# Six pairs instead of four in five output chunks of a one-layer encoder, with the last norm's weight row in its own tile

## The chip, the cores and the metric

The kernel runs on one core of one Trainium2 chip (trn2). The core's engines run side by side, each with its own in-order list of instructions, and wait for each other through semaphores: TensorE (PE, matmuls, with its weight loads as PEld), VectorE (DVE), ScalarE (ACT), GpSimd (POOL) and SyncE (SP), which issues nearly all DMAs. The metric is the device time of one execution in microseconds; lower is better.

## The reference

One layer: an embedding norm, one large input projection, two branches (a gated short convolution and banded window attention), one output projection, and a norm over the sum with the scaled stream. All in float32, 256 tokens by 4096 columns.

```python
h = layer_norm(x, emb_ln_g, emb_ln_b)
p = h @ w_in                       # 4096 x 13312
y_conv = c_b * centred_short_conv(c_c * c_h, conv_w) * silu(c_z)
y_attn = banded_window_attention(a_q, a_k, a_v, sink) * silu(a_z)
y = concatenate([y_conv, y_attn]) @ w_out      # 4096 x 4096
out = layer_norm(2 ** 0.25 * h + y, ln_g, ln_b)
```

## The kernel before, in words

**Two halves of a number.** TensorE multiplies rounded float32. To keep precision, each weight and each activation is split into a high half (rounded) and a low half (the rest), and three products are summed: high by high, activation's low by weight's high, activation's high by weight's low. ScalarE writes a weight's high half `whi` (line 226), VectorE its low half `wlo` (line 230), and TensorE takes both.

**Steps.** The whole work is one list of steps, `steps`, built from strings (lines 45 to 49). A letter `s` is a *piece*: 4 row blocks of 128 weights by 512 columns, 1 MB, 32 matmuls with the high half and 16 with the low (`mm_out`, line 957, in the output projection). A letter `S` is a *pair*: 2 row blocks by 512 columns, 0.5 MB, multiplied by a scheme of seven products instead of eight (`mm_pair`, lines 300 to 303): 14 matmuls with high halves and 7 with low. Four row blocks are thus one piece (48 matmuls) or two pairs (42). A pair costs more elsewhere: sums of its weight blocks on VectorE (`sums`, lines 192 to 194 for two neighbouring pairs in one go, 205 to 207 for a single one), sums of the activations for its row blocks, made once for all chunks (`x_sums`, called from `y_sums`), and a combination of the products at the end of the chunk (`pair_sums`, lines 709 to 712).

**Coupled pairs.** Two pairs that stand next to each other in the list are a couple. Both their weights lie in the four slots of the tile `wall`, and their sums are one set of three instructions (lines 192 to 194) that needs both loads. A couple may not use the extra load buffers that lie in the result tile `R` (R0 and R1 up to chunk 4, R2 in chunks 5 and 6); pieces and single pairs may.

**The output projection.** 4096 columns are nine chunks, numbered 0 to 8: seven of 512 columns, two of 256. Chunks 0 and 1 are eight pieces each, chunks 2 to 6 follow the string `sSsSsSsSss`, chunks 7 and 8 are pieces. In this document a chunk's steps are counted from 0.

**What one step issues, in this order.** For step j: its matmuls; on ScalarE the high halves of step j + 3; whatever is due `later`; then `loads(j)` puts weight loads up to seven steps ahead on SP, each waiting until its buffer's last user is split; on VectorE the block sums of step j + 4 if that is a pair, then the low halves of step j + 3. There are three buffers for high halves and three for low ones, so both of step j + 3 wait for TensorE to be through with step j. Behind these come, in certain steps of a chunk: the residual (`residual`, lines 938 and 940: the stream's norm for the chunk's columns), the product with the last norm's weight row for the chunk before (`end_out2`, line 979), and the loads of the residual's rows (`res_load`, lines 928 to 932). After the last step comes the chunk's end (`end_out`, lines 972 to 975: sum and statistics).

**The last norm's rows.** In step 4 of chunk 2 `rows_load` fetches the last norm's weights and biases; in step 8 `rows_split` splits them on VectorE (lines 904 and 905) and sends them with 15 small DMAs on SP (line 908) to the tile `rows`, used at the very end.

Of the kernel before, what the change touches and what calls it, by code (L numbers as in the profile page):

```python
# [8 lines left out]
F32 = mybir.dt.float32  # L9
F32R = mybir.dt.float32r  # L10
AF = mybir.ActivationFunctionType
ALU = mybir.AluOpType
AX = mybir.AxisListType

P = 128
# [26 lines left out]
HT = S // 2  # L42
# [2 lines left out]
PAIRS = [0, 0, NP1] + [NP] * (len(IN_ORDER) - 3)  # L45
ORDERS = {0: "s" * 8, NP1: "sssSSsSsSs", NP: "sSSsSSSSsSSs"}
OUT = 100
OP = 4
OUT_ORDERS = ["s" * 8] * 2 + ["sSsSsSsSss"] * 5 + ["", ""]
N_W = 4  # L50
OFF = 4
GAP = 64
# [20 lines left out]
def out_units(n):  # L73

    if CHUNKS[n] < W:
        return [("out", OUT + n, q) for q in range(KT * CHUNKS[n] // PIECE)]
    q, p, us = 2 * npairs(OUT + n) // PK, 0, []
    for u in OUT_ORDERS[n]:
        if u == "s":
            us.append(("out", OUT + n, q))  # L80
            q += 1
        else:
            us.append(("opair", OUT + n, p))
            p += 1
    assert q == NPC
    return us


def npairs(ci):
    return PAIRS[ci] if ci < OUT else OUT_ORDERS[ci - OUT].count("S")  # L90

# [3 lines left out]
N_IN = len(IN_STEPS)  # L95
# [6 lines left out]
def encoder_kernel(ctx: ExitStack, tc: tile.TileContext, x, emb_g, emb_b, wi, ws, conv_w, sink, wo, ln_g, ln_b, out):  # L102
    nc = tc.nc
# [14 lines left out]
    steps = IN_STEPS + OUT_STEPS  # L118
    chunks = []
# [4 lines left out]
    def couple(j):  # L124
# [5 lines left out]
    psc = pw = pc = R = None  # L130
    extra = []
    user = {}
    in_R = [(steps.index(("opair", OUT + 4, OP - 1)) + 1, "R0"), (steps.index(("opair", OUT + 4, OP - 1)) + 1, "R1"),
            (steps.index(("opair", OUT + 6, OP - 1)) + 1, "R2")]

    def w_bufs(j):

# [86 lines left out]
    def split_hi(j):  # L224
        wh[j] = half_tile(j, "whi")
        nc.scalar.activation(part(j, wh[j]), part(j, raw[j]), AF.Copy)  # L226
# [24 lines left out]
    for name in ("whi", "wall", "wlo0", "m", "nm", "wlo1", "den", "es", "wlo2"):  # L251
        n = {"whi": PIECE + GAP}.get(name, PIECE + 2 * OFF if name[:3] == "wlo" else N_W * PIECE if name == "wall" else 2)
        t = wpool.tile([P, n], F32, name=name, bufs={"whi": 3, "m": 4, "nm": 3, "den": 4, "es": 3}.get(name, 1))
# [25 lines left out]
    pacc, SC = {}, None  # L279
# [211 lines left out]
    SC = [sc_tiles[p // (NP - 3)][:, p % (NP - 3), :, :, :] for p in range(NP)]  # L491
# [208 lines left out]
    def pair_copy(ci):  # L700
        e = st_["e", ci] = sum_tile(ci)
        nc.scalar.activation(e[:, 0, 0:HW], pacc[ci, 0][:, 0, :], AF.Copy)
# [86 lines left out]
    def at(j, fn, *a):  # L789
        later.setdefault(j, []).append((fn, a))  # L790
# [71 lines left out]
    ncs = len(chunks)  # L862
    res = {}
    p2 = st2 = ms2 = rows = t5 = lhs5 = None
    RB = [(0, 0), (0, 1), (0, 2), (32, 0), (32, 1), (32, 2), (64, 0), (64, 1)]

    def bcast(src, a, n):
        return bass.AP(tensor=src.tensor, offset=src.offset + a, ap=[[0, P], [1, n]])
# [22 lines left out]
    def z_tile():  # L891
        if not zt:
            zt.append(p2.tile([P, 12 * W], F32, name="z", tag="SC"))
        return zt[0]
# [15 lines left out]
    def res_load(n):  # L910
        if n >= ncs:
            return
        c0, w, _, _ = chunks[n]
        if n < ncs - 1:
            gb = p2.tile([P, 3, w], F32, name="gb")
        if n < ncs - 2:
            xc = p2.tile([P, 2, W], F32, name="xc")[:, :, 0:w]
        elif n == ncs - 2:
            xc = z_tile()[:, 6 * W:6 * W + 2 * w].rearrange("p (a b) -> p a b", a=2)
        else:  # L920
            z = zt[0]
            gb = z[:, 0:3 * w].rearrange("p (a b) -> p a b", a=3)
            xc = z[:, 3 * w:5 * w].rearrange("p (a b) -> p a b", a=2)
            g1, b1, t1 = (z[:, 5 * w + k * W:5 * w + (k + 1) * W] for k in range(3))
            first_cols.extend((g1, b1, t1, z[:, 5 * w + 3 * W:5 * w + 3 * W + P]))
            nc.sync.dma_start(out=g1, in_=bcast(ln_g, 0, W))
            nc.sync.dma_start(out=b1, in_=bcast(ln_b, 0, W))
        nc.sync.dma_start(out=gb[:, 0, :], in_=bcast(emb_gr, c0, w))
        nc.sync.dma_start(out=gb[:, 1, :], in_=bcast(emb_br, c0, w))
        nc.sync.dma_start(out=gb[:, 2, :], in_=bcast(ln_g, c0, w))  # L930
        for i in range(2):
            nc.sync.dma_start(out=xc[:, i, :], in_=x[i * P:(i + 1) * P, c0:c0 + w])
        res[n] = gb, xc

    def residual(n):
        gb, xc = res[n]
        for i in range(2):
            nc.vector.scalar_tensor_tensor(xc[:, i, :], xc[:, i, :], musd[:, i, 0:1], gb[:, 0, :],
                                           op0=ALU.subtract, op1=ALU.mult)
            nc.vector.scalar_tensor_tensor(xc[:, i, :], xc[:, i, :], musd[:, i, 2:3], gb[:, 1, :],  # L940
                                           op0=ALU.mult, op1=ALU.add)
# [34 lines left out]
        return r  # L976

    def end_out2(n, i, r):
        nc.vector.tensor_tensor(r, r, res[n][0][:, 2, :], op=ALU.mult)

    def finish_lhs(n, i):
        r = end_out(n, i)
# [53 lines left out]
    def y_sums(k):  # L1036
        nonlocal SC
        if k == 0:
            t = p2.tile([P, 6, 2, 4, HT], F32R, name="SCy", tag="SC")
            SC = [t[:, p, :, :, :] for p in range(OP)]  # L1040
        x_sums(k, R[:, 0, 2 * W:4 * W])

    for k in range(OP):
        at(chunks[1][3] + 1 + k, y_sums, k)
    ends = []
    for n, (c0, w, pk, j0) in enumerate(chunks):
        us = out_units(n)
        np_ = sum(u[0] == "opair" for u in us)
        for t, (kind, _, q) in enumerate(us):
            j = j0 + t  # L1050
            if kind == "opair":
                mm_pair(j)
            else:
                mm_out(j, n, (0,) if n == ncs - 1 else (0, 1))
            if j + 3 < len(steps):
                split_hi(j + 3)
            for fn, a in later.pop(j, []):
                fn(*a)
            if kind == "opair" and q == np_ - 1:
                pair_copy(OUT + n)  # L1060
                at(j + 1, pair_sums, OUT + n)
                at(j + 1, plus_res, n)
            if j == N_IN + 5:
                open_p2()
            loads(j)
            if j == N_IN + 5:
                res_load(0)
            sums(j + 4)
            if j + 3 < len(steps):
                split_lo(j + 3)  # L1070
            if t == 0 and n:
                for a in ends:
                    end_out2(*a)
                ends = []
                if n < ncs - 1:
                    res_load(n)
            if t == (0 if n == ncs - 1 else 2 if n == ncs - 2 else 4 if n else 7):
                residual(n)
            if n == 2 and t == 4:
                rows_load()  # L1080
            if n == 2 and t == 8:
                rows_split()
                nc.scalar.activation(small.tile([P, 1], F32, name="sd", bufs=1), eps_t, AF.Abs_reciprocal_sqrt)
            if n == ncs - 2 and t == 1:
                res_load(ncs - 1)
        if n < ncs - 1:
            ends = [(n, i, end_out(n, i)) for i in range(2)]
    assert not later
    last_mm = chunks[-1][3]
    n = ncs - 1  # L1090
# [78 lines left out]
```

## Time and profile before

| | |
|---|---|
| median of 3 runs | 1501.05 us (1500.09 to 1501.15) |
| profiled execution | 1500.92 us |
| its span, first to last instruction | 1499.2 us |
| TensorE busy | 1482.4 us |
| VectorE busy | 1338.4 us |
| ScalarE busy | 803.3 us |
| output chunk 2 begins, chunk 3 begins | 1229.7 us, 1271.9 us |

How to read the profile: a row of the order of time gives start and length in us, engine, line, operation, what it writes and reads, and in square brackets the idle time of the engine before it and what ended that. A row of a stretch gives, engine by engine, busy us and the number of instructions; then TensorE's granted clock as a share of full speed, the mean busy share of the 16 DMA engines, and GB/s. A row of a group gives busy us, the mean ns of one, and idle time before it. SPq is SP's queue: its rows are the issuing of DMAs, not their transfer.

### The profile page before, as it was taken

The numbers are of one execution on the slowest core, as the hardware profiler recorded it, in microseconds if no ns is written. First come the engines' busy times: TensorE is split into PE (matmuls) and PEld (weight loads), VectorE is DVE, ScalarE is ACT, GpSimd is POOL, SyncE is SP. The second block draws the span as 40 slices with busy tenths as digits, with TensorE's granted clock in tenths as the row PEclk, the third lists the DMA queues.
The fourth block names the chain that finished last, engine by engine and source line by source line (L and its number), as shares of the span: only waits on it lengthen the run. The fifth ranks groups of instructions, "written<-read, shape, count | busy, mean of one in ns | idle before, by whom it ended". The sixth has DMA issues, their size and how long they took to land.

```text
span 1499.2 us, 29810 instructions
## 1 busy us (share of the span) xinstructions
PE 1482.4 (99%) x12878; PEld 1465.4 (98%) x12878; DVE 1338.4 (89%) x1384; ACT 803.3 (54%) x687; POOL 1.3 (0%) x7
## 2 busy tenths in 40 slices
PE   7999999999999999999999999999999999999998
PEld 4999999999999999999999999999999999999997
DVE  7768999898999999999999999999998688888876
ACT  5544656766666665655555555555555444444431
POOL 0000000000000000000000000000000000000000
PEclk9999999999999999999999999999999999999999
DMA  8545465555554556646545655556558656756663
GB/s 318 217 183 196 164 217 189 192 197 208 180 204 176 190 201 209 230 177 224 200 182 219 231 198 197 225 204 241 191 207 313 233 201 220 290 215 230 219 237 113
DMA packets 71365, 316.17 MB, mean 211 GB/s; under 512 B 8545, under 2 KB 12609, under 8 KB 50113
## 3 DMA queue, kind: packets, MB, share of 16 engines
q1 hardware_dynamic: 70224, 312.43, 57.3%
q8 instruction: 101, 1.65, 0.4%
q10 hardware_dynamic: 1008, 1.84, 0.3%
q14 instruction: 32, 0.25, 0.0%
HBM read 305.23 MB, written 8.91 MB: 210 GB/s over the span
## 4 chain that ended last, share of the span: by engine, by line
PE 93%; DVE 3%; ACT 1%; issue 1%; DMA 1%; SPq 0%; ACTq 0%; DVEq 0%
PE acc L275 39%; PE acc L957 20%; PE pacc L301 6%; PE pacc L300 6%; PE pacc L303 6%; PE acc L301 4%; PE acc L300 4%; PE acc L303 4%; DVE wlo L230 1%; PE att L518 1%; ACT whi L226 1%; DVE st L354 0%; PE acc L404 0%; DMA wall<-in_ws 0%; DVE wall L192 0%
## 5 line engine op out<-in xcount | busy, mean ns | idle before, releaser
L226 ACT ACTIVATE whi<-wall 128x1792 fp32r<-128x1792 f32 (+1 forms) x284 | 501.7, 1772 | 464.6 <-DVE wall L194 149.7
L230 DVE TENSOR_TENSOR wlo<-wall,whi 128x1792 fp32r<-128x1792 f32 (+1 forms) x284 | 593.4, 2096 | 75.9 <-ACT whi L226 64.3
L275 PE MATMUL acc<-whi,xT 128*128 128x256 f32 x3584 | 427.6, 276 | 0.0
L275 PEld LDWEIGHTS acc<-whi,xT 128*128 128x128 f32 x3584 | 415.8, 188 | 0.0
L275 PE MATMUL acc<-wlo,xT 128*128 128x256 f32 x1792 | 221.3, 275 | 0.0
L275 PEld LDWEIGHTS acc<-wlo,xT 128*128 128x128 f32 x1792 | 211.4, 188 | 0.0
L226 ACT ACTIVATE whi<-w 128x2048 fp32r<-128x2048 f32 x73 | 140.7, 1927 | 114.6 <-PE acc L275 72.5
L957 PE MATMUL acc<-whi,xT 128*128 128x256 f32 x1696 | 201.8, 275 | 0.0
L957 PEld LDWEIGHTS acc<-whi,xT 128*128 128x128 f32 x1696 | 196.6, 188 | 0.4 <-issue 0.4
L230 DVE TENSOR_TENSOR wlo<-w,whi 128x2048 fp32r<-128x2048 f32 x73 | 166.8, 2286 | 10.8 <-ACT whi L226 10.6
L192 DVE TENSOR_TENSOR wall<-wall 128x1024 f32<-128x1024 f32 x93 | 113.3, 1218 | 11.0 <-DMA wall<-in_ws 8.7
L300 PE MATMUL acc<-whi,xT 128*128 128x256 f32 x416 | 114.7, 276 | 0.0
L301 PE MATMUL acc<-whi,xT 128*128 128x256 f32 x416 | 114.6, 276 | 0.0
L300 PE MATMUL pacc<-whi,xT 128*128 128x256 f32 x396 | 111.0, 280 | 0.0
L303 PE MATMUL pacc<-wlo,xT 128*128 128x256 f32 x396 | 109.2, 276 | 0.6 <-DVE wlo L230 0.4
L301 PE MATMUL pacc<-whi,xT 128*128 128x256 f32 x396 | 109.1, 276 | 0.0
L957 PE MATMUL acc<-wlo,xT 128*128 128x256 f32 x848 | 105.3, 275 | 0.0
L303 PE MATMUL acc<-wlo,xT 128*128 128x256 f32 x416 | 104.4, 275 | 0.0
L300 PE MATMUL pacc<-whi,SC 128*128 128x256 f32 x376 | 103.6, 275 | 0.0
L301 PE MATMUL pacc<-whi,SC 128*128 128x256 f32 x376 | 103.6, 275 | 0.0
L957 PEld LDWEIGHTS acc<-wlo,xT 128*128 128x128 f32 x848 | 100.4, 188 | 0.0
L303 PE MATMUL pacc<-wlo,SC 128*128 128x256 f32 x376 | 94.5, 276 | 0.0
(224 smaller groups left out, 1930.1 us busy)
## 6 DMA issues: line engine op xcount, KB each, us to landing
wall<-in_ws SPq DMA_DIRECT2D x202, 512.0 KB
w<-in_wi SPq DMA_DIRECT2D x73, 1024.0 KB
wall<-in_wo SPq DMA_DIRECT2D x43, 1024.0 KB
wall<-in_wi SPq DMA_DIRECT2D x39, 1024.0 KB
R<-in_wo SPq DMA_DIRECT2D x10, 1024.0 KB
x<-in_x SPq DMA_DIRECT2D x7, 512.0 KB
yl<-yd SPq DMA_DIRECT2D x7, 512.0 KB
xc<-in_x SPq DMA_DIRECT2D x14, 256.0 KB
```

Of the source, the lines that this page charges most:

```text
L192: nc.vector.tensor_tensor(t[:, :, 4:6, :], t[:, :, 1:3, :], t[:, :, 0:1, :].to_broadcast([P, 2, 2, HW]), op=ALU.add)
L226: nc.scalar.activation(part(j, wh[j]), part(j, raw[j]), AF.Copy)
L230: nc.vector.tensor_tensor(part(j, wl[j]), part(j, raw[j]), part(j, wh[j]).bitcast(F32), op=ALU.subtract)
L275: nc.tensor.matmul(acc[ci, i][:, c:c + HW], x, w[:, k * W + c:k * W + c + HW], start=(first and w is hi and k + off + c == 0), stop=(last ...
L300: nc.tensor.matmul(o, ah, hi[:, w, :], start=(opens and p == 0), stop=False)
L301: nc.tensor.matmul(o, al, hi[:, w, :], start=False, stop=False)
L303: nc.tensor.matmul(o, ah, lo[:, w, :], start=False, stop=(closes and last))
L518: nc.tensor.transpose(ps[:, c, i * P:(i + 1) * P], t[:, i, (2 * b + c) * P:(2 * b + c + 1) * P], ident)
L957: nc.tensor.matmul(acc[ci, i][:, c:c + HW], y, m[:, k * w + c:k * w + c + HW], start=(first and off + c == 0), stop=(last and c + HW == w))
```

## The change

Chunks 2 to 6 follow `sSSsSSsSSss`: eleven steps, five pieces and six pairs, all of the pairs in couples. The activation sums of six pairs are made instead of four, in the last two steps of chunk 0 and the first four of chunk 1 (before: steps 1 to 4 of chunk 1). The last norm's weight row gets a tile of its own, `lg`, with two buffers; the residual's other two rows stay in `gb`. For chunks up to 6 the product with the weight row moves from step 0 to step 3 and the residual from step 4 to step 6; the residual's loads stay in step 0.

```diff
-OP = 4
-OUT_ORDERS = ["s" * 8] * 2 + ["sSsSsSsSss"] * 5 + ["", ""]
+OP = 6
+OUT_ORDERS = ["s" * 8] * 2 + ["sSSsSSsSSss"] * 5 + ["", ""]
...
-    in_R = [(steps.index(("opair", OUT + 4, OP - 1)) + 1, "R0"), (steps.index(("opair", OUT + 4, OP - 1)) + 1, "R1"),
-            (steps.index(("opair", OUT + 6, OP - 1)) + 1, "R2")]
+    in_R = [(steps.index(("opair", OUT + 4, npairs(OUT + 4) - 1)) + 1, "R0"), (steps.index(("opair", OUT + 4, npairs(OUT + 4) - 1)) + 1, "R1"),
+            (steps.index(("opair", OUT + 6, npairs(OUT + 6) - 1)) + 1, "R2")]
...
-            gb = p2.tile([P, 3, w], F32, name="gb")
+            gb = p2.tile([P, 2, w], F32, name="gb")
+            lg = p2.tile([P, w], F32, name="lg", bufs=2)
...
-            gb = z[:, 0:3 * w].rearrange("p (a b) -> p a b", a=3)
+            gb = z[:, 0:2 * w].rearrange("p (a b) -> p a b", a=2)
+            lg = z[:, 2 * w:3 * w]
...
-        nc.sync.dma_start(out=gb[:, 2, :], in_=bcast(ln_g, c0, w))
+        nc.sync.dma_start(out=lg, in_=bcast(ln_g, c0, w))
...
-        nc.vector.tensor_tensor(r, r, res[n][0][:, 2, :], op=ALU.mult)
+        nc.vector.tensor_tensor(r, r, res[n][2], op=ALU.mult)
...
-            t = p2.tile([P, 6, 2, 4, HT], F32R, name="SCy", tag="SC")
+            t = p2.tile([P, OP, 2, 4, HT], F32R, name="SCy", tag="SC")
...
-        at(chunks[1][3] + 1 + k, y_sums, k)
+        at(N_IN + 6 + k, y_sums, k)
...
-            if t == 0 and n:
+            if t == (3 if n < ncs - 2 else 0) and n:
                 for a in ends:
                     end_out2(*a)
                 ends = []
-                if n < ncs - 1:
-                    res_load(n)
-            if t == (0 if n == ncs - 1 else 2 if n == ncs - 2 else 4 if n else 7):
+            if t == 0 and 0 < n < ncs - 1:
+                res_load(n)
+            if t == (0 if n == ncs - 1 else 2 if n == ncs - 2 else 6 if n else 7):
                 residual(n)
```

How the instructions stand, on SP around the 15 small DMAs (`rows`). In these rows `in_wo` is the pieces' weights, `in_ws` the pairs', `wall` and `R` the buffers they go to, `gb`, `lg` and `xc` the residual's rows. Before:

```order
L172 DMA wall<-in_ws 128x1024
L908 DMA rows<-R 1x12x128 x6
L908 DMA rows<-R 1x8x128 x3
L908 DMA rows<-R 1x12x128 x4
L908 DMA rows<-R 1x8x128 x2
L172 DMA wall<-in_wo 128x2048
L172 DMA wall<-in_ws 128x1024
L928 DMA gb<-in_emb_g_row 128x512
```

Now:

```order
L172 DMA wall<-in_ws 128x1024
L908 DMA rows<-R 1x12x128 x6
L908 DMA rows<-R 1x8x128 x3
L908 DMA rows<-R 1x12x128 x4
L908 DMA rows<-R 1x8x128 x2
L172 DMA wall<-in_ws 128x1024
L172 DMA R<-in_wo 128x2048
L172 DMA wall<-in_ws 128x1024
L930 DMA gb<-in_emb_g_row 128x512
```

Before, the two loads behind the 15 were those of chunk 3's step 6 (a piece) and step 7 (a pair). Now the load just ahead of them is the first pair of the couple of chunk 3's steps 4 and 5, and the one just behind them is the second; the piece of step 6 and the first pair of the next couple follow.

On VectorE, from the rows' split in chunk 2 (L904, L905) into chunk 3. `wlo` rows are the low halves, 128x2048 of a piece and 128x1792 of a pair. Before:

```order
L905 TENSOR_TENSOR R<-R 32x128
L205 TENSOR_TENSOR R<-R 128x512
L206 TENSOR_TENSOR R<-R 128x256
L207 TENSOR_TENSOR R<-R 128x256
L230 TENSOR_TENSOR wlo_14381<-wall,whi 128x2048
L972 TENSOR_TENSOR R<-acc,R 128x512
L975 BN_STATS s_13291<-R 128x6
L972 TENSOR_TENSOR R<-acc,R 128x512
L975 BN_STATS s_13292<-R 128x6
L230 TENSOR_TENSOR wlo_14440<-R,whi 128x1792
L979 TENSOR_TENSOR R<-R,gb 128x512 x2
L205 TENSOR_TENSOR wall<-wall 128x512
```

Now, from the end of chunk 2:

```order
L974 TENSOR_TENSOR R<-acc,R 128x512
L977 BN_STATS s_13291<-R 128x6
L974 TENSOR_TENSOR R<-acc,R 128x512
L977 BN_STATS s_13292<-R 128x6
L192 TENSOR_TENSOR wall<-wall 128x2x512
L193 TENSOR_TENSOR wall<-wall 128x2x256
L194 TENSOR_TENSOR wall<-wall 128x2x256
L230 TENSOR_TENSOR wlo_14453<-R,whi 128x2048
L230 TENSOR_TENSOR wlo_14489<-wall,whi 128x1792
L230 TENSOR_TENSOR wlo_14515<-wall,whi 128x1792
```

In step 0 of chunk 3 there stand now the sums of the couple of steps 4 and 5 (L192 to L194), ahead of the low half of step 3's piece (`wlo_14453`); before, step 0 held one pair's low half and the product with the weight row, and single pairs' sums came one by one.

More of the change, by code (lines that the diff above doesn't have):

```diff
@@ L929, in res_load @@
         nc.sync.dma_start(out=gb[:, 1, :], in_=bcast(emb_br, c0, w))
-        nc.sync.dma_start(out=gb[:, 2, :], in_=bcast(ln_g, c0, w))
+        nc.sync.dma_start(out=lg, in_=bcast(ln_g, c0, w))
         for i in range(2):
             nc.sync.dma_start(out=xc[:, i, :], in_=x[i * P:(i + 1) * P, c0:c0 + w])
-        res[n] = gb, xc
+        res[n] = gb, xc, lg
     def residual(n):
-        gb, xc = res[n]
+        gb, xc, _ = res[n]
         for i in range(2):
```

## The prediction

> **What bounds the kernel now.** I read the engines' shares first, then the chain of waits, then two stretches by engine.
>
> ```profile
> PE 1482.4 (99%) x12878; PEld 1465.4 (98%) x12878; DVE 1338.4 (89%) x1384; ACT 803.3 (54%) x687; POOL 1.3 (0%) x7
> PE 93%; DVE 3%; ACT 1%; issue 1%; DMA 1%; SPq 0%; ACTq 0%; DVEq 0%
> core 0: us, PE busy (x) PEld busy (x) DVE busy (x) ACT busy (x) POOL busy (x), PEclk, DMA share, GB/s
> 672.00:755.00 83.00, 83.00 (x734) 83.00 (x733) 78.61 (x64) 44.52 (x28) 0.00 (x0) 1.00 0.60 216
> 1272.00:1314.00 42.00, 42.00 (x373) 42.00 (x372) 37.08 (x40) 18.49 (x12) 0.00 (x0) 1.00 0.68 266
> ```
>
> TensorE (PE) is busy 1482 of 1499 us and carries 93% of the chain. The stretch 1272 to 1314 is output chunk 3: 42.00 of 42.00 us busy, no hole, clock 1.00. So only fewer matmuls can shorten this part, and only if whatever feeds TensorE stays ahead. Next to it stands VectorE (DVE): 37.08 of 42 us here, and 78.61 of 83 us (94.7%) in two input chunks that already use eight pairs each, where TensorE still has no hole. VectorE at 95% is therefore no reason for a stall by itself.
>
> **What the change removes.** In chunk 0 every step is a piece of 48 matmuls. These two rows of VectorE's order of time are splits of two consecutive steps, each ending a wait that TensorE's pace sets:
>
> ```profile
> 1181.10 2.29 DVE L230 TENSOR_TENSOR wlo<-wall,whi 128x2048 fp32r<-128x2048 f32 x1 [3.10 <-ACT whi L226]
> 1186.54 2.29 DVE L230 TENSOR_TENSOR wlo<-wall,whi 128x2048 fp32r<-128x2048 f32 x1 [3.15 <-ACT whi L226]
> ```
>
> They start 5.44 us apart, so a matmul takes 5.44 / 48 = 0.1133 us, a piece 5.44 us, a pair of 21 matmuls 2.38 us. A chunk goes from 6 x 48 + 4 x 21 = 372 matmuls (42.16 us) to 5 x 48 + 6 x 21 = 366 (41.48 us). Five chunks: 30 x 0.1133 = **3.40 us less**, if TensorE never waits. That is 0.23%; a difference under 0.2% (3.0 us) can't be told from none here.
>
> **What it adds on VectorE.** Durations are taken from start to next start, since that is what an in-order queue costs:
>
> ```profile
> 1080.84 1.21 DVE L192 TENSOR_TENSOR wall<-wall 128x1024 f32<-128x1024 f32 x1
> ...
> 1083.42 2.28 DVE L230 TENSOR_TENSOR wlo<-w,whi 128x2048 fp32r<-128x2048 f32 x1
> 1085.63 2.02 DVE L230 TENSOR_TENSOR wlo<-wall,whi 128x1792 fp32r<-128x1792 f32 x1
> 1087.56 0.48 DVE L744 SCALAR_TENSOR_TENSOR t<-att,cw,t 128x255 f32<-128x255 f32 x1
> ...
> 1238.58 0.68 DVE L205 TENSOR_TENSOR wall<-wall 128x512 f32<-128x512 f32 x1
> ```
>
> ```profile
> 1197.68 0.68 DVE L675 TENSOR_TENSOR R<-xT 128x512 f32<-128x512 f32 x1
> ...
> 1200.73 2.28 DVE L230 TENSOR_TENSOR wlo<-R,whi 128x2048 fp32r<-128x2048 f32 x1
> ...
> 1237.37 1.29 DVE L979 TENSOR_TENSOR R<-R,gb 128x512 f32<-128x512 f32 x2
> ...
> 1240.10 2.28 DVE L230 TENSOR_TENSOR wlo<-wall,whi 128x2048 fp32r<-128x2048 f32 x1
> ...
> 1253.01 0.74 DVE L938 SCALAR_TENSOR_TENSOR xc<-xc,musd,gb 128x512 f32<-128x512 f32 x1
> ...
> 1255.91 2.28 DVE L230 TENSOR_TENSOR wlo<-R,whi 128x2048 fp32r<-128x2048 f32 x1
> ...
> 1265.16 0.41 DVE L709 TENSOR_TENSOR R<-R,pacc 128x256 f32<-128x256 f32 x1
> ...
> 1268.06 2.02 DVE L230 TENSOR_TENSOR wlo<-wall,whi 128x1792 fp32r<-128x1792 f32 x1
> 1270.00 0.21 DVE L904 CAST R<-R 32x128 fp32r<-32x128 f32 x1
> ...
> 1274.61 0.68 DVE L972 TENSOR_TENSOR R<-acc,R 128x512 f32<-128x512 f32 x1
> ...
> 1277.59 2.02 DVE L230 TENSOR_TENSOR wlo<-R,whi 128x1792 fp32r<-128x1792 f32 x1 [0.25 <-PE acc L957]
> ```
>
> Split of a piece: 2.21 us (1083.42 to 1085.63). Split of a pair: 1.93. Block sums of two coupled pairs: 2.58 (1080.84 to 1083.42); of a single pair: 1.52 (1238.58 to 1240.10). The stream's residual row: 2.90 (1253.01 to 1255.91). Pair combination plus adding the residual: 2.90 (1265.16 to 1268.06). Chunk end: 2.7 (1274.61 to 1277.59 less the wait of 0.25). Weight-row product: 1.21 (1237.37 to 1238.58). A chunk before: 6 x 2.21 + 4 x 1.93 + 4 x 1.52 + 9.7 = 36.8 us, against 37.08 in the stretch above, which also holds about 1 us of the last norm's rows. After: 5 x 2.21 + 6 x 1.93 + 3 x 2.58 + 9.7 = **40.1 us of 41.48**. That fits, with 1.4 us to spare.
>
> Within a chunk the splits can't run ahead of TensorE: a low-half buffer is free only when the step three back is done. So VectorE falls behind while four pairs pass and catches up at the long pieces. Counted from a chunk's start: TensorE ends step 6 at 25.84 (4 pairs, 3 pieces); from there VectorE has 0.3 lag, a split 2.21, residual 2.90, split 2.21, couple sums 2.58, split 2.21, combination 2.90, two pair splits 3.86, chunk end 2.7, together 21.9, so it is done at 47.7, 6.2 us into the next chunk. There: couple sums to 8.8, the split for step 3 to 11.0 (TensorE asks at 10.20 + 3.63 = 13.8), two pair splits to 14.9 (17.2 and 19.6), sums 17.5, split 19.7 (24.0), product 20.9, two pair splits 24.8 (27.4 and 29.8); at 25.84 it waits for TensorE again. The smallest room is 2.8 us, so work alone stalls nothing. The product and residual in later steps keep off the first splits of a chunk; with the weight row in its own tile the residual's loads no longer wait for that product. I price both at nothing: they lie under TensorE, and if that cover were gone they would be 1.21 and 2.90 us a chunk.
>
> The x sums of two more pairs are 2 x 3.05 us (1197.68 to 1200.73) in chunks 0 and 1. There VectorE has a split and one such sum per step: 2.21 + 3.05 = 5.26 of 5.44 us. The one step that also has residual and chunk end puts it some 8 us behind; a piece's split has about 12 us of room. Nothing lost.
>
> **The wait that it adds.** The last norm's rows are split in step 8 of chunk 2, and then 15 small DMAs go out on SP, the one queue for weight loads:
>
> ```profile
> 1270.23 11.50 SPq L908 DMA_DIRECT2D rows<-R  x15
> 1281.83 0.39 SPq L172 DMA_DIRECT2D wall<-in_wo  x1
> 1282.32 0.37 SPq L172 DMA_DIRECT2D wall<-in_ws  x1
> 1289.07 0.69 DVE L205 TENSOR_TENSOR wall<-wall 128x512 f32<-128x512 f32 x1 [1.63 <-DMA wall<-in_ws]
> ```
>
> They hold the queue 11.6 us (1270.23 to 1281.83). Behind them stood, before, the loads of chunk 3's step 6 (a piece) and step 7 (a pair), whose sums are due only in step 3 of that chunk; even so VectorE waited 1.63 us for the second, while TensorE had no hole. After: the first load behind the 15 is the *second of the couple of chunk 3's steps 4 and 5*. Both pairs' sums are one set of instructions, they stand at step 0 of chunk 3, and ahead of the low split of its step 3. VectorE is in order: until that load lands, the split that TensorE needs next cannot start.
>
> The clock of it, from Z = TensorE ends step 6 of chunk 2 (VectorE is idle there, some 2 us ahead):
> - VectorE: 0.3 lag (the 0.25 above), split 2.21, residual 2.90, split 2.21, couple sums 2.58, split 2.21, cast 0.23 (1270.00 to the first issue): Z + 12.6.
> - SP: 11.6 for the 15: Z + 24.2. Then the pair's load is issued.
> - Landing. No row has it alone. The nearest:
>
> ```profile
> 676.76 0.38 SPq L172 DMA_DIRECT2D wall<-in_ws  x1
> 681.39 1.23 DVE L192 TENSOR_TENSOR wall<-wall 128x1024 f32<-128x1024 f32 x1 [0.34 <-DMA wall<-in_ws]
> ```
>
> 4.6 us from issue to use, with a store issued 0.4 us before it; at most 6.7 us (1282.32 to 1289.07) behind a load twice its size; not under 0.5 MB / 424 GB/s, some 1.2 us plus a start. I take 3.8, near the 4.6 less that store: Z + 28.0.
> - Couple sums 2.58, split 2.28: Z + 32.9.
> - TensorE: steps 7 to 10 of chunk 2 take 2 x 2.38 + 2 x 5.44 = 15.64; chunk 3's steps 0 to 2 10.20; the high half of step 3 (32 matmuls) 3.63. It asks for the low half at Z + 29.5.
>
> Stall: **3.4 us** (2.0 for a landing in 2.4, 4.2 for 4.6). Afterwards the next couple's load stands behind the residual loads; by the same sums the next piece's split is about 0.8 us early, so up to 1 us more if that load is late.
>
> [...]
>
> **Sum.** 1500.92 (profiled execution: span 1499.2 and 1.7 around it) - 3.40 + 3.4 = 1500.9. The median of the three runs is 0.13 above that execution: **1501.0 us**. The gain of 30 matmuls is given back in one place.
>
> **Rivals.**
> 1. *The 15 DMAs delay nothing.* For: before, the same block cost TensorE nothing. Against: then no couple stood right behind it. It needs the load 3.4 us earlier. Then all 3.40 stays: 1501.05 - 3.40 = 1497.6. Chance 0.10.
> 2. *The stall halves TensorE's clock.* After the last matmul the granted clock falls:
>
> ```profile
> 1494.80:1499.20 4.40, 0.00 (x0) 0.00 (x0) 0.00 (x0) 0.58 (x1) 0.00 (x0) 0.78 0.57 214
> L417 PE MATMUL att<-x,ident 128*128 128x512 f32 x4 | 3.8, 1094 | 8.4 <-DMA x<-in_x 8.4
> L1031 PE MATMUL acc<-R,z 128*128 128x512 f32 x6 | 3.4, 644 | 0.0
> ```
>
> 0.78 over 4.4 us is half speed for the last 1.9 us, so it fell 2.5 us after the work ended. A stall of 3.4 us is longer than that; whether it counts depends on how it lies. The first four matmuls of the kernel took 1094 ns against 644 ns for the same shape later, over 3.8 us: about half of that, 1.8 us, is the price. 1502.8, still no change. Chance 0.32. [...]
> 3. *VectorE becomes the bound* (the other side: slower). It has 1.4 us spare per chunk. In chunks 5 and 6 a couple's second load waits for a buffer freed only one split before, and I get waits of about 1.7 us there, which the room at step 6 takes up. If the four chunks 3 to 6 each wait 3 us for loads, each is 40.1 + 3.0 - 41.5 = 1.6 us longer: 1501.0 + 6.4 = 1507.4. It decides from waits of 1.4 us in every chunk on, less what the room takes. For: 1.63 us of such a wait already. Against: the 94.7% stretch without a hole. Chance 0.12.
>
> That fewer matmuls are not issued can be left out: the new order of steps fixes the count.
>
> **Numbers.** My forecast 0.46, rivals 0.10, 0.32, 0.12. Faster by over 0.2% is rival 1: 0.10; slower by over 0.2% is rival 3: 0.12; the rest, 0.78, lies within. Range 1499.3 (landing in 2.4 us) to 1503.2 (the clock, and a later second load).
>
> **What would show it.** Right: 30 fewer matmuls; chunks 4 to 6 at 41.5 us each; one hole in TensorE of 3 to 4 us, in chunk 3, at the low half of its first piece after a couple, released by VectorE's split; before it VectorE idle some 5 us on the sums of a couple, ended by a weight load that was issued right after the 15. Wrong: no such hole and 1497.6; holes in every chunk; or a hole elsewhere. A clock below 1.00 after the hole is rival 2.

## The result and the profile after

| | before | after |
|---|---|---|
| median of 20 executions each | 1500.95 us (1500.09 to 1501.71) | 1502.71 us (1501.56 to 1504.68) |
| ratio | | 1.0014, 95% interval 1.0008 to 1.002 |
| profiled execution, its span | 1500.92, 1499.2 us | 1502.21, 1500.5 us |

The changed kernel is slower by 0.14%. That is under the 0.2% that the prediction called no change, but the whole interval lies above 1: what came is the second rival (1502.8), not the forecast (1501.0). Two executions of the experiments below, of 1534.58 and 3263.86 us, were slow ones, and the medians and ranges leave them out.

The engines' shares and the chain of waits of the changed kernel:

```profile
PE 1480.6 (99%) x12848; PEld 1463.4 (98%) x12848; DVE 1357.8 (90%) x1386; ACT 809.5 (54%) x694; POOL 1.3 (0%) x7
PE 91%; DVE 5%; issue 1%; DMA 1%; ACT 1%; SPq 0%; DVEq 0%; ACTq 0%
```

There are 30 matmuls fewer (12878 to 12848), but TensorE's busy time falls by 1.8 us, not by 3.4: some matmuls have become longer. VectorE's share of the chain goes from 3% to 5%; there is now a place where TensorE waits for it. That place stands in the order of time. First SP's queue, where the 15 small DMAs go out:

```profile
1267.45 11.60 SPq L908 DMA_DIRECT2D rows<-R  x15
1279.15 0.38 SPq L172 DMA_DIRECT2D wall<-in_ws  x1
...
1281.01 0.50 SPq L931 DMA_DIRECT2D gb<-in_emb_b_row  x1
1281.55 0.44 SPq L932 DMA_DIRECT2D lg<-in_ln_g  x1
...
1283.07 0.43 SPq L172 DMA_DIRECT2D wall<-in_ws  x1
```

The 1279.15 row is the second load of the couple of chunk 3's steps 4 and 5; the 1283.07 row is that of the next couple, behind the residual's loads. VectorE, which needs both:

```profile
1276.92 0.70 DVE L977 BATCH_NORM_STATS2 s<-R 128x6 f32<-128x512 f32 x1
1282.49 1.23 DVE L192 TENSOR_TENSOR wall<-wall 128x1024 f32<-128x1024 f32 x1 [4.87 <-DMA wall<-in_ws]
...
1285.09 2.29 DVE L230 TENSOR_TENSOR wlo<-R,whi 128x2048 fp32r<-128x2048 f32 x1
1287.29 3.95 DVE L230 TENSOR_TENSOR wlo<-wall,whi 128x1792 fp32r<-128x1792 f32 x2
1294.14 1.23 DVE L192 TENSOR_TENSOR wall<-wall 128x1024 f32<-128x1024 f32 x1 [2.90 <-DMA wall<-in_ws]
```

And TensorE at step 3 of chunk 3, high half and low half, then the next pair's first matmuls:

```profile
1280.61 3.79 PE L959 MATMUL acc<-whi,xT 128*128 128x256 f32 x32
1287.43 2.85 PE L959 MATMUL acc<-wlo,xT 128*128 128x256 f32 x16 [3.03 <-DVE wlo L230]
1290.07 0.41 PE L300 MATMUL pacc<-whi,xT 128*128 128x256 f32 x1
```

VectorE stands idle for 4.87 us until the couple's load is there, splits at 1285.09, and TensorE goes on at 1287.43. From 1280.61 the 32 high matmuls need 3.63 us at the usual spacing; the low half begins 6.82 us later, so the hole is 3.19 us. Behind it, 16 low matmuls show 2.85 us; behind the shorter holes of kernels below, 2.12. The stretches say why: the columns are as in the prediction, PEclk the granted clock, for 3.4 us behind the hole and for the three chunks after it:

```profile
1288.60:1292.00 3.40, 3.40 (x19) 3.40 (x18) 2.64 (x2) 1.82 (x2) 0.00 (x0) 0.50 1.06 409
1317.00:1358.40 41.40, 41.40 (x368) 41.40 (x367) 40.90 (x39) 20.20 (x13) 0.00 (x0) 1.00 0.72 245
1358.40:1399.80 41.40, 41.40 (x368) 41.40 (x367) 39.61 (x37) 19.87 (x13) 0.00 (x0) 1.00 0.64 236
1399.80:1441.20 41.40, 41.40 (x367) 41.40 (x366) 39.73 (x36) 20.11 (x13) 0.00 (x0) 1.00 0.72 264
```

TensorE gets half its clock for 3.4 us, although it is busy all that time. It does the work of some 1.7 us in 3.4, so this costs some 1.7 us. Chunks 4 to 6 have no hole.

**Where the time went.** I take the output projection from its first matmul to its last in chunk 8, and the tail from there to the span's end, both read off each trace's order of time on TensorE. The output projection lasts 344.14 us before and 345.74 us after: -3.40 for the matmuls, +3.19 for the hole, and the +1.8 that remain for the clock (1.7 by the row above), together +1.6. The tail lasts 13.28 before and 13.82 after, +0.54. Together 1500.95 + 2.1 = 1503.1; measured 1502.71. All that stands ahead of the output projection, which the change does not touch, was 0.8 us shorter in the profiled execution (1140.95 us for 1141.74); in a second profile (the experiment "The changed kernel once more") it was 0.5 us longer, so I count that as scatter.

### The profile page after: what moved, and what is told of

Same layout as the page of the kernel before. It is cut to its first block, busy times and chain, and to the rows that moved or that the text cites. A ratio compares the mean times of both kernels' runs of the same rounds, so it can differ in the third digit from the quotient of the medians.

```text
span 1500.5 us, 29780 instructions
## 1 busy us (share of the span) xinstructions
PE 1480.6 (99%) x12848; PEld 1463.4 (98%) x12848; DVE 1357.8 (90%) x1386; ACT 809.5 (54%) x694; POOL 1.3 (0%) x7
## 4 chain that ended last, share of the span: by engine, by line
PE 91%; DVE 5%; issue 1%; DMA 1%; ACT 1%; SPq 0%; DVEq 0%; ACTq 0%
PE acc L275 39%; PE acc L959 16%; PE pacc L301 6%; PE pacc L300 6%; PE pacc L303 6%; PE acc L301 5%; PE acc L300 5%; PE acc L303 5%; DVE wlo L230 2%; PE att L518 1%; DVE st L354 0%; PE att L648 0%; DVE wall L192 0%; PE acc L404 0%; PE att L634 0%
## 5 line engine op out<-in xcount | busy, mean ns | idle before, releaser
L226 ACT ACTIVATE whi<-wall 128x1792 fp32r<-128x1792 f32 (+1 forms) x290 | 508.6, 1762 | 462.8 <-DVE wall L194 195.5
L230 DVE TENSOR_TENSOR wlo<-wall,whi 128x1792 fp32r<-128x1792 f32 (+1 forms) x290 | 601.9, 2086 | 48.6 <-ACT whi L226 47.9
L275 PEld LDWEIGHTS acc<-whi,xT 128*128 128x128 f32 x3584 | 415.8, 188 | 0.0
L275 PEld LDWEIGHTS acc<-wlo,xT 128*128 128x128 f32 x1792 | 211.4, 188 | 0.0
L959 PEld LDWEIGHTS acc<-whi,xT 128*128 128x128 f32 x1536 | 178.1, 188 | 0.4 <-issue 0.4
L192 DVE TENSOR_TENSOR wall<-wall 128x1024 f32<-128x1024 f32 x108 | 131.7, 1220 | 21.1 <-DMA wall<-in_ws 16.9
L300 PE MATMUL pacc<-whi,xT 128*128 128x256 f32 x406 | 113.8, 280 | 0.0
L301 PE MATMUL pacc<-whi,xT 128*128 128x256 f32 x406 | 112.0, 276 | 0.0
L959 PEld LDWEIGHTS acc<-wlo,xT 128*128 128x128 f32 x768 | 91.6, 189 | 3.2 <-DVE wlo L230 3.2
```

The costliest lines, as they stand in the source:

```text
L192: nc.vector.tensor_tensor(t[:, :, 4:6, :], t[:, :, 1:3, :], t[:, :, 0:1, :].to_broadcast([P, 2, 2, HW]), op=ALU.add)
L230: nc.vector.tensor_tensor(part(j, wl[j]), part(j, raw[j]), part(j, wh[j]).bitcast(F32), op=ALU.subtract)
L275: nc.tensor.matmul(acc[ci, i][:, c:c + HW], x, w[:, k * W + c:k * W + c + HW], start=(first and w is hi and k + off + c == 0), stop=(last ...
L300: nc.tensor.matmul(o, ah, hi[:, w, :], start=(opens and p == 0), stop=False)
L301: nc.tensor.matmul(o, al, hi[:, w, :], start=False, stop=False)
L959: nc.tensor.matmul(acc[ci, i][:, c:c + HW], y, m[:, k * w + c:k * w + c + HW], start=(first and off + c == 0), stop=(last and c + HW == w))
```

## The experiments

The theory after the result: the 15 small DMAs delay one load, this makes one hole, the hole halves the clock, and nothing else has changed. Its rivals: the side edits cost something; VectorE has too little room in every chunk; the clock's share is wrong and the rest is scatter. Each kernel is the changed one with the edit shown, but for the fourth experiment, and each is compared with the kernel before on the same chip. No kernel leaves work out; two add matmuls whose product nobody reads.

### The 15 DMAs on another queue

```diff
-                    nc.sync.dma_start(out=rows[b + r:b + r + 1, 0:n * P].bitcast(F32), in_=hl[a0:a0 + n, h, :].bitcast(F32))
+                    nc.gpsimd.dma_start(out=rows[b + r:b + r + 1, 0:n * P].bitcast(F32), in_=hl[a0:a0 + n, h, :].bitcast(F32))
```

> The changed kernel, but the 15 small DMAs of the last norm's rows go out on GpSimd's queue instead of SP's. Theory (the 15 stand ahead of the couple's second load on SP, VectorE waits for that load, TensorE for VectorE, and the idle time halves the clock): the hole in chunk 3 and the half-speed stretch go, the 30 matmuls less remain: 1502.7 - 3.2 - 1.8 = 1497.7 us, no hole of TensorE after 1225 us. Rival (VectorE is simply too full with six pairs, or the moved residual makes it late): a hole of 2 to 3 us stays, 1502 us.

Measured: 1498.03 us (1497.14 to 1498.93), ratio 0.9981 (0.9972 to 0.999). The output projection lasts 340.76 us, 3.38 less than before, without a hole. GpSimd's queue in that place:

```profile
1269.20 4.26 POOL L908 DMA_DIRECT2D rows<-R  x8 [1202.22 <-DVE R L905]
1276.04 0.52 POOL L908 DMA_DIRECT2D rows<-R  x1 [2.58 <-DMA rows<-R]
1276.79 3.07 POOL L908 DMA_DIRECT2D rows<-R  x6 [0.23 <-DVE R L974]
```

The same 15 DMAs go out where no weight load waits behind them. All else of the change is still there, so what makes the hole and the slow clock is the place of the 15 in SP's queue.

### The 15 DMAs three at a time

They stay on SP, three in each of five steps.

```diff
+    row_dmas = []
+    def rows_send(k):
+        for o, i in row_dmas[:k]:
+            nc.sync.dma_start(out=o, in_=i)
+        del row_dmas[:k]
...
-                    nc.sync.dma_start(out=rows[b + r:b + r + 1, 0:n * P].bitcast(F32), in_=hl[a0:a0 + n, h, :].bitcast(F32))
+                    row_dmas.append((rows[b + r:b + r + 1, 0:n * P].bitcast(F32), hl[a0:a0 + n, h, :].bitcast(F32)))
...
+            if row_dmas:
+                rows_send(3 if n == 2 and t == 8 else 3)
```

> The changed kernel, but the 15 small DMAs are sent three at a time, at the end of five steps (8 to 10 of chunk 2, 0 and 1 of chunk 3), still on SP. Theory (what costs is 11.6 us of one queue in one piece): each group of three holds SP 2.3 us, less than the room of the loads: no hole, 1497.7 us. Rival (any use of SP there delays the loads, or the small transfers disturb the large ones): 1499 to 1502.7 us.

Measured: 1497.08 us (1496.38 to 1497.88), ratio 0.9976 (0.9966 to 0.9985): faster than both kernels. The output projection lasts 340.74 us, 3.40 less than before, as summed from the 30 matmuls. SP's queue, then VectorE's one wait there:

```profile
1272.96 2.31 SPq L905 DMA_DIRECT2D rows<-R  x3
1275.31 0.51 SPq L172 DMA_DIRECT2D R<-in_wo  x1
1275.86 2.03 SPq L905 DMA_DIRECT2D rows<-R  x3
1278.00 0.38 SPq L172 DMA_DIRECT2D wall<-in_ws  x1
```

```profile
1290.38 1.23 DVE L192 TENSOR_TENSOR wall<-wall 128x1024 f32<-128x1024 f32 x1 [2.44 <-DMA wall<-in_ws]
```

A load now waits behind three small DMAs (2.3 us) and not behind 15. The wait of 2.44 us on VectorE is for the next couple's load; it costs TensorE nothing, so there are at least 2.4 us of room at that place.

### The old order with the side edits alone

The kernel before, with the tile `lg`, the later product and residual, and the earlier activation sums:

```diff
-            gb = p2.tile([P, 3, w], F32, name="gb")
+            gb = p2.tile([P, 2, w], F32, name="gb")
+            lg = p2.tile([P, w], F32, name="lg", bufs=2)
...
-        at(chunks[1][3] + 1 + k, y_sums, k)
+        at(N_IN + 6 + k, y_sums, k)
...
-            if t == 0 and n:
+            if t == (3 if n < ncs - 2 else 0) and n:
...
-            if t == (0 if n == ncs - 1 else 2 if n == ncs - 2 else 4 if n else 7):
+            if t == (0 if n == ncs - 1 else 2 if n == ncs - 2 else 6 if n else 7):
```

> The changed kernel with the old order of steps and four pairs: only the weight row's own tile, the later product, the later residual and the earlier activation sums are left of the change. Theory (these lie under TensorE): 1501.0 us, as before, no hole. Rival (the later residual and product delay the splits and share in the loss): 1501.5 us or more, a hole in chunks 2 to 6.

Measured: 1500.88 us (1500.21 to 1501.42), ratio 1.0001 (0.9992 to 1.001), output projection 344.14 us as before. VectorE waits behind the same 15 DMAs here too:

```profile
1291.40 0.69 DVE L205 TENSOR_TENSOR wall<-wall 128x512 f32<-128x512 f32 x1 [3.85 <-DMA wall<-in_ws]
```

3.85 us, longer than the 1.63 before, and TensorE has no hole. The side edits cost nothing in the old order, where the load behind the 15 is due late enough.

### Seventeen in front

Two of the DMAs are sent twice. With `rows_send` as above:

```diff
+            if n == 2 and t == 8:
+                row_dmas[0:0] = row_dmas[0:2]
+                rows_send(17)
```

> The changed kernel with 17 small DMAs in a row on SP: the first two are sent twice, with the same data. The couple's second load is issued 1.6 us later. Theory: the hole is 4.8 us, the clock falls as before: 1.6 us more than the changed kernel, 1504.1 us. Rival (another limit than SP's queue sets the hole): no more than 0.3 us above the changed kernel's 1502.5 us.

Measured: 1506.58 us (1504.97 to 1508.81), ratio 1.004 (1.0028 to 1.0053). TensorE's low half of step 3, SP's queue, and the clock in two stretches:

```profile
1291.75 3.78 PE L966 MATMUL acc<-wlo,xT 128*128 128x256 f32 x16 [6.42 <-DVE wlo L230]
```

```profile
1268.38 15.03 SPq L905 DMA_DIRECT2D rows<-R  x17
1283.51 0.38 SPq L172 DMA_DIRECT2D wall<-in_ws  x1
```

```profile
1285.33:1291.75 6.42, 0.00 (x1) 0.00 (x1) 4.87 (x5) 2.09 (x2) 0.00 (x0) 0.83 0.91 347
1289.50:1296.40 6.90, 4.65 (x22) 4.65 (x23) 6.06 (x3) 5.09 (x3) 0.00 (x0) 0.51 0.86 306
```

The size missed: the queue is held for 15.03 us, 3.4 us more and not the 1.6 us of the two issues that I had added. At the 0.77 us of one of the 15 (11.6 / 15) 17 issues are 13.1 us, so 1.9 us are left over, for which no row names the cause. For the theory that serves as well: 3.4 us more in the queue lengthen the hole by 3.4 (3.19 to 6.58 by the matmuls' starts), one for one.

### Thirteen in front

13 of the 15 where they were, two in step 5 of chunk 3:

```diff
+            if n == 2 and t == 8:
+                rows_send(13)
+            if n == 3 and t == 5:
+                rows_send(15)
```

> The changed kernel with 13 of the 15 small DMAs where they are and the last two sent in step 5 of chunk 3. The couple's second load is issued 1.3 us earlier. Theory (wait and clock): the hole falls from 3.2 to 1.9 us, too short for the clock to fall, so both go: 1500.8 - 3.4 + 1.9 = 1499.3 us, clock 1.00 throughout. Rival (the clock's fall costs nothing in the end, only the length of the wait counts): 1.3 us less than the changed kernel, 1501.2 us.

Measured: 1501.58 us (1500.29 to 1502.5), ratio 1.0004 (0.9996 to 1.0013), 2.3 us over what I expected. TensorE in chunk 3:

```profile
1286.95 2.12 PE L966 MATMUL acc<-wlo,xT 128*128 128x256 f32 x16 [1.62 <-DVE wlo L230]
...
1298.56 2.13 PE L966 MATMUL acc<-wlo,xT 128*128 128x256 f32 x16 [1.10 <-DVE wlo L230]
```

The first hole is 1.4 us shorter, and there is a second one, where the next couple's load stands behind the residual's loads. In the changed kernel that load is as late, but the first hole and the slow clock have put TensorE 5 us back, and so it isn't missed. This is the prediction's "up to 1 us more"; it measures 1.27 us by the matmuls' starts, a little over that.

### The residual's loads later

Those of chunk 3 go out in step 2 and not in step 0, so that the next couple's load stands ahead of them.

```diff
-            if t == 0 and 0 < n < ncs - 1:
+            if t == (2 if n == 3 else 0) and 0 < n < ncs - 1:
```

> The changed kernel with the loads of chunk 3's residual rows issued in step 2 of that chunk instead of step 0, behind the next couple's loads. It takes away the second wait of VectorE (2.9 us for the load of the couple of steps 7 and 8) and leaves the first. Theory: the hole of 3.2 us and the half-speed stretch stay, 1502.3 us; the second wait is worth little, since the half-speed stretch covers it. Rival (the second wait is a good part of the loss): 1501 us or less.

Measured: 1503.35 us (1501.49 to 1504.09), ratio 1.0015 (1.0006 to 1.0024). VectorE's second wait is gone, the first hole is as before, and so is the clock behind it:

```profile
1288.24 3.50 PE L959 MATMUL acc<-wlo,xT 128*128 128x256 f32 x16 [3.01 <-DVE wlo L230]
```

```profile
1287.80:1291.20 3.40, 2.96 (x14) 2.96 (x15) 3.40 (x3) 3.40 (x3) 0.00 (x0) 0.51 0.55 188
```

The executions fall into two groups by their mean clock: three at 1.000 took 1501.49 to 1501.89 us (mean 1501.69), eight at 0.998 or 0.999 took 1502.61 to 1504.09 (mean 1503.50). The same kernel thus seems to pay 1.8 us for the clock in most executions and nothing in some. The mean clock tells this only at its ends: 0.999 stands on profiled executions with the slow stretch ("The changed kernel once more") and without it (eleven in front, below), while no kernel without a hole has an execution at 0.998 or less.

### Matmuls in the hole

Twelve matmuls on constants, which appear as 24 records, fill the wait ahead of the low half of that step:

```diff
+            if m is lo and n == 3 and j == j0 + 3:
+                busy = ps_att.tile([P, P], F32, name="att")
+                for _ in range(12):
+                    nc.tensor.matmul(busy, ident, ident, start=True, stop=True)
```

> The changed kernel with 12 matmuls of a constant 128x128 tile added between the high and the low half of step 3 in chunk 3, where TensorE waits 3.2 us; they fill about 2.8 us of that wait and their result is not used. Theory (the wait costs 3.2 us, and 1.8 us more because the idle time halves the clock): the clock stays at 1.00 and the time falls by 1.8 to 1500.9 us, the wait's 3.2 us stay. Rival (the clock's drop is only seen in this execution, or costs nothing since VectorE is behind anyway): 1502.7 us, no change.

Measured: 1502.46 us (1501.88 to 1504.13), ratio 1.0012 (1.0004 to 1.0021): not the gain of the clock that I expected. TensorE:

```profile
1288.28 2.12 PE L963 MATMUL acc<-wlo,xT 128*128 128x256 f32 x16 [0.34 <-DVE wlo L230]
...
1299.02 2.12 PE L963 MATMUL acc<-wlo,xT 128*128 128x256 f32 x16 [0.24 <-DVE wlo L230]
...
1424.32 1.90 PE L963 MATMUL acc<-wlo,xT 128*128 128x256 f32 x14 [0.48 <-DVE wlo L230]
```

The clock is 1.00 throughout (2.12 us for 16 matmuls, not 2.85), but the time comes back elsewhere: 2.76 us of added matmuls and a rest of 0.50, then 0.41 at the next couple, then 0.65 in chunk 6. There VectorE stood idle for 2.41 us ahead of a couple's sums, 1.30 us in the changed kernel; the profile doesn't name what ended it, but the couple's second load had gone out only 4.3 us before. The output projection is 1.35 us longer than before, against 1.60 without the added matmuls. By itself this run could not tell the clock's price from a second wait.

### Matmuls in the hole, and the residual's loads later

Both edits:

> The one before, with the 12 constant matmuls in the wait of chunk 3's step 3 that keep TensorE's clock up. With the second wait gone nothing else can take the place of the half-speed stretch. Theory (the clock's fall costs 1.8 us of its own): 1.8 us less than the one before, 1500.5 us. Rival (the clock's fall costs nothing in the end): the same as the one before, 1502.3 us.

Measured: 1501.66 us (1500.55 to 1502.38), ratio 1.0005 (0.9996 to 1.0014). With the second wait out of the way, TensorE:

```profile
1288.58 2.12 PE L963 MATMUL acc<-wlo,xT 128*128 128x256 f32 x16 [0.59 <-DVE wlo L230]
```

The clock stays at 1.00, the hole with its filling is 3.5 us, and the median is 1.7 us below that of the kernel without the matmuls and level with its three executions that kept the clock. That is the price of the clock, by itself: 1.7 to 1.8 us, as the prediction's second rival had it.

### Thirteen, then eleven in front, and the residual's loads later

> Both edits together: 13 of the 15 small DMAs ahead and two later, and chunk 3's residual rows loaded two steps later. The first hole is then about 1.8 us, too short for the clock, and VectorE's second wait is gone. Theory (three terms: the first wait, the second wait of 1.3 us that stands behind it, the clock): 1501.0 - 3.4 + 1.8 = 1499.4 us, to 0.5 more where the load lands late. Rival (the second wait was not what kept the run with 13 at 1501.6): 1501.4 us.

Measured with 13: 1501.61 us (1499.87 to 1503.17), ratio 1.0003 (0.9994 to 1.0012). The profiled execution took 1499.87 us, with one hole and no second one:

```profile
1286.86 2.12 PE L966 MATMUL acc<-wlo,xT 128*128 128x256 f32 x16 [1.62 <-DVE wlo L230]
```

```profile
1286.90:1294.00 7.10, 7.10 (x62) 7.10 (x63) 7.03 (x6) 3.27 (x3) 0.00 (x0) 1.00 0.75 230
```

The profiled execution agrees with the expectation and the median doesn't. By mean clock, three executions at 1.000 took 1499.87 to 1500.79 us, three at 0.998 took 1501.46 to 1502.47, and four at 0.999, which can be either, 1500.18 to 1503.17. So the clock seems to fall behind a hole of 1.8 us too, in some executions; no profile shows it, so this is argued from the clocks, not shown.

With eleven (`rows_send(11)`, the other four in step 5 of chunk 3):

> Eleven of the 15 small DMAs ahead of the couple's second load, four in step 5 of chunk 3, and the residual's loads of chunk 3 in step 2. My theory (the hole is as long as the queue's delay less the room there was): 13 ahead left a hole of 1.79 us, two fewer shift the load by 2 x 0.77 = 1.55 us, so a hole of 0.0 to 0.5 us is left, too short for the clock, and the median is 1497.6 to 1498.2 us. Rival (executions with the couple differ by something other than the hole, as the median of 13 ahead, 1.9 us above its own profiled sum, would have it): again about 2 us above the sum, 1499.5 us or more.

Measured: 1498.98 us (1498.39 to 1500.53), ratio 0.9988 (0.9979 to 0.9997). VectorE's wait:

```profile
1281.01 1.23 DVE L192 TENSOR_TENSOR wall<-wall 128x1024 f32<-128x1024 f32 x1 [1.97 <-DMA wall<-in_ws]
```

The hole left is 0.29 us, as expected, and the clock stays. The median is 0.8 us above my upper end, half a microsecond below what the rival wanted at least. By the one profile, 0.6 us of that lies behind the output projection, in the tail (below).

### Three at a time, and the residual's loads later

> The changed kernel with the small DMAs sent three at a time over five steps, and chunk 3's residual rows loaded two steps later. Theory (no hole is left to remove): the same as with the small DMAs spread alone, 1497.4 us, no hole of TensorE in the output projection. Rival (VectorE's wait of 2.4 us that the spread alone still shows costs something in other executions): 0.5 us less, 1496.8 us.

Measured: 1497.00 us (1496.57 to 1497.58), ratio 0.9974 (0.9964 to 0.9983), not to be told from the 1497.08 of three at a time alone; output projection 340.74 us, as there. VectorE's wait of 2.44 us is gone, and no time with it: it had been covered.

### The changed kernel once more

> The changed kernel once more, for a second profile of the same place. If the hole's length comes from the order of the queue alone, it is 3.0 to 3.4 us again; if the load's landing changes from execution to execution, it differs by up to 1 us. The clock at half speed behind it: in about 8 of 11 executions by the clocks of the kernel with the later residual loads, so probably again 3.4 us of it; time 1502 to 1504 us.

Measured: 1503.41 us in one execution. TensorE and the stretch behind the hole:

```profile
1288.63 3.30 PE L959 MATMUL acc<-wlo,xT 128*128 128x256 f32 x16 [2.94 <-DVE wlo L230]
```

```profile
1289.30:1292.70 3.40, 3.40 (x18) 3.40 (x17) 3.15 (x2) 2.34 (x2) 0.00 (x0) 0.51 0.95 355
```

The hole is 3.10 us, against 3.19 and 3.17 in the two other profiles with 15 in front: it comes from the order of the queue, and scatters little.

### All runs in one sum

To the median before of each batch I add the difference of the output projection and that of the tail, both from the one profile of each kernel:

| kernel | output projection | tail | sum | median |
|---|---|---|---|---|
| changed kernel | +1.60 | +0.54 | 1503.1 | 1502.71 |
| GpSimd's queue | -3.38 | +0.34 | 1497.7 | 1498.03 |
| three at a time | -3.40 | -0.48 | 1496.9 | 1497.08 |
| side edits alone | 0.00 | +0.01 | 1500.8 | 1500.88 |
| matmuls in the hole | +1.35 | +0.51 | 1502.6 | 1502.46 |
| 13 in front | +0.04 | +0.40 | 1501.4 | 1501.58 |
| 17 in front | +5.49 | +0.06 | 1506.5 | 1506.58 |
| residual later | +1.29 | +0.42 | 1502.7 | 1503.35 |
| residual later, matmuls | +0.17 | +0.43 | 1501.6 | 1501.66 |
| residual later, 13 | -1.46 | +0.41 | 1499.9 | 1501.61 |
| residual later, 11 | -2.95 | +0.61 | 1498.4 | 1498.98 |
| residual later, three at a time | -3.40 | -0.37 | 1497.2 | 1497.00 |

Nine of twelve medians lie within 0.4 us of the sum. The one that is far off, 13 with the residual later, has a profile with the clock kept and three executions whose mean clock says that they lost it. So what the kernels differ by lies in the output projection and the tail. The sums don't say what is in the output projection; that no chunk pays for a full VectorE is shown by chunks 4 to 6 above, where TensorE is busy for 41.40 of 41.40 us.

## Why the prediction was wrong, step by step

- **The 30 matmuls, -3.40 us: right.** Without a hole the output projection is 3.38 to 3.40 us shorter, in three kernels.
- **VectorE's room of 1.4 us a chunk: right.** It is busy 39.6 to 40.9 of 41.40 us in chunks 4 to 6, where 40.1 of 41.48 had been summed, and TensorE has no hole there. Rival 3 did not come.
- **The wait behind the 15 DMAs: right in place, cause and size.** With Z at 1254.77 (chunk 3's start at 1270.41 less 15.64), the forecast had the load issued at Z + 24.2 and it went at Z + 24.4; the landing was taken as 3.8 us, and from issue to use it took 3.3 (the 424 GB/s in its lower bound is what the DMA engines moved in the kernel before from 8.00 to 10.00 us); the low half was to start at Z + 32.9 and started at Z + 32.7. Stall 3.19 us for 3.4. The two experiments without the block ahead of the load show the cause, and the 17 show the size one for one. Rival 1 did not come.
- **"Up to 1 us more" for the next couple's load: there, but hidden.** In the changed kernel the first hole covers it. Where the first hole was shortened or filled, it came out with 1.27 and 0.41 us.
- **The side edits at nothing: right**, by the kernel that has them alone (ratio 1.0001, 0.9992 to 1.001).
- **The clock: here it failed.** The forecast took it as likelier (0.46 to 0.32) that TensorE's clock survives a stall of 3.4 us. It fell, in all three profiles of a hole of 3.1 to 3.2 us, and stayed at half for 3.4 us; the price, put at nothing in the sum, is 1.7 to 1.8 us, as the rival had it. The evidence for it stood in the prediction: the clock had fallen 2.5 us after the last matmul, in the same kernel, and a stall of 3.4 us is longer. "Whether it counts depends on how it lies": the runs show that it doesn't count in every execution (three of the eleven with the residual later are at 1.000), but at this length it counts in most: of the changed kernel's 20, 12 have a mean clock of 0.998 or 0.997, and none has 1.000. That it is the way it lies which decides is an estimate, from the stretches in the last section.
- **The tail, +0.5 us: not in the sum at all.** I took all behind the last chunk as unchanged, since the change doesn't touch it. What the engines do there is unchanged; the last store lands later.
- **How close the rival came is in part luck.** Its 1502.8 has neither the tail's +0.5 us nor a stall of 3.19, and the sum with both is 1503.1; measured was 1502.71. And the lower end of the range, 1499.3, is 0.3 us under what its own terms give: 1500.9 - 3.4 + 2.0 + 0.1 = 1499.6.

An idle time of 2.94 to 3.03 us lost the clock each time it was profiled: 3.03 us in the changed kernel, 2.94 in its second profile, 3.01 with the residual later.

## What to carry to other kernels

When an order of steps is changed, look at what now stands right behind every block of small DMAs on an in-order queue, and when its reader needs it; here 11.6 us of issuing, harmless in the old order, met a load with 3 us too little room, and spreading the block three at a time gave back 5.0 us in the output projection. Price a hole in TensorE as the hole plus what the clock loses behind it, if it is about as long as the holes here: an idle time of 3.0 us lost the clock in most executions, and with 1.62 us both profiles kept it, though other executions seem to have lost it. And before shortening a hole, look for the next wait behind it: a long hole hides the lateness of whatever comes after.

## What the runs showed of the hardware

**The clock.** Behind a hole it fell 2.6 to 4.2 us after TensorE went idle: with the residual later at 1287.8, while TensorE still stood idle from 1285.23; in the changed kernel at 1288.6, when it had been idle from 1284.40 and busy again for 1.2 us. At the end of the kernel before it fell at 1497.27, 2.5 us after the last matmul had ended at 1494.74. It stayed at half (0.50) for 3.4 us behind the holes of 3.1 to 3.2 us, and for 6.8 us behind the hole of 6.58 us; no profile shows a length between.

Two traces, of the kernel before and of the changed kernel, show where it changed. The changed kernel has 1.00 for 1276.585 us from 12.005, where its record of the clock begins, to 1288.59, then 0.50 for 3.413 us, then 1.00 for 204.800 us and 0.50 from 1496.80. The kernel before has 1.00 for 1484.798 us from 12.476, where its record begins, to 1497.27. So each stretch that ended within these two executions lasted a whole number of times 3.4133 us: 374, 1 and 60 in the changed kernel, 435 in the kernel before. In the three profiles that lost the clock behind a hole of 3.1 to 3.2 us, TensorE had been busy for 0.6 to 1.2 of the 3.4 us before the fall. With 13 in front and the residual later it was idle for 1.62 us, thus busy for 1.8 us or more of any 3.4 us there, and the clock stayed at 1.00. How much it takes is not settled: at the end of the changed kernel, among other matmuls, the clock fell at 1496.80, behind 3.41 us with 2.18 us busy. Nor is it shown why executions of one kernel differ; that it hangs on how a hole lies to such multiples of 3.4133 us is my estimate from these stretches.

**The tail.** The last store to the output (256 KB, issued on ACT) lands 2.35 us after its issue before, and 3.44 us after it in the changed kernel. From there to the end it takes 1.40 us before and 0.84 us in the changed kernel, so the tail is longer by 0.54 us and not by 1.09. The DMA engines between the two, before, in the changed kernel, with three at a time, and with eleven in front, each from the store's issue to its landing in 40 slices:

```profile
GB/s 383 558 349 314 453 453 209 454 384 279 453 314 279 523 418 244 453 488 209 419 454 314 349 488 453 314 418 383 314 418 314 70 0 0 0 0 0 0 0 0
```

```profile
GB/s 381 381 405 381 357 381 381 262 357 405 405 333 381 381 405 405 357 333 381 357 262 191 24 95 0 24 24 24 0 24 24 24 24 24 0 0 0 0 0 0
q14 instruction: 2, 0.02, 1.2%
```

```profile
GB/s 305 508 406 237 440 474 305 339 441 372 271 474 271 339 508 440 203 440 474 305 305 508 440 305 339 440 440 271 406 271 136 34 0 135 135 0 0 0 0 0
q14 instruction: 2, 0.02, 1.8%
```

```profile
GB/s 350 420 373 397 374 374 374 280 420 373 350 397 327 397 374 397 350 373 327 373 304 24 0 93 0 0 23 23 23 0 23 23 47 23 0 0 0 0 0 0
q14 instruction: 2, 0.02, 1.9%
```

In the changed kernel nine slices at 24 GB/s close the transfer: in slices of 0.086 us that is one packet of 2 KB each, which looks like the last of one engine's share. Two packets of the queue that loads instructions (8 KB; 1.2% of 16 times 3.44 us, 0.33 us each) come there too, one just ahead of these slices and one among them (the 95). With three at a time the same two packets stand behind all data (the two slices at 135), before none falls into this time, and there the store lands in 2.42 and 2.35 us. With eleven in front two such packets come before the landing as well (1.9% of 16 times 3.51 us, 0.53 us each), one of them among the last slices (the 93), and the store lands after 3.51 us. So it seems that a store at the very end can be a microsecond later because code is loaded while its last packets are on their way. That the two fall into the same time is what these four traces show, and no more: whether one DMA engine carries both they don't tell, why they meet in one build and not in another I haven't found, and that the packets cause the whole microsecond is argued from these cases, not shown.
